# Hi/lo pieces of a token mixer's weights: made in the first feed-forward's input stage and kept in DRAM, instead of beside the projections and the attention that use them

## The chip, the cores and the metric

The kernel runs on one core of one Trainium2 chip. The metric is device microseconds from the start to the end of the launch. The kernel before took 1909.49 us as the median of three runs (1908.7 to 1911.0). The execution that the profile shows took 1910.44 us.

## What is computed

One layer of a hybrid encoder on a sequence of 1024 tokens with 1024 features, all in float32. Three sub-layers follow one another, each with a modulation by a condition vector `c` and a layer norm behind it:

```python
x = post_norm(x, mod[0], 0.5, swiglu(h, ffn1_w_in, ffn1_w_out))
x = post_norm(x, mod[1], 1.0, hybrid_mixer(h, mix_w_in, ..., mix_w_out))
x = post_norm(x, mod[2], 0.5, swiglu(h, ffn2_w_in, ffn2_w_out))
# post_norm: layer_norm(ALPHA*x + w*(1 + gate(c)) * f(x*(1 + scale(c)) + shift(c)))
```

The mixer has one input projection. 1024 of its columns feed a gated unit and a depthwise convolution of width 31; 3 x 512 columns are queries, keys and values of a differential attention (two softmax maps for each of four heads). The two halves are concatenated, and `mix_w_out`, scaled by `1 + gate(c)`, maps them to the output.

## The kernel before

**Arithmetic.** TensorE multiplies in a rounded float32 format. So that the product keeps float32's accuracy, each operand is split into a rounded part `hi` (a copy on ACT) and the rest `lo` (a subtraction on DVE or POOL), and each product is made of three matmuls: hi x hi, hi x lo, lo x hi. `split` (L140) is that pair of instructions. Of a weight that means a load, an ACT copy and a subtraction before TensorE can use it.

**Stages.** Feed-forward 1 has an input stage (`in_phase(0, ...)`, pool `p1a`) and an output stage (`out_phase(0, ...)`, pool `p1b`); then come the mixer's gated unit and its projections (pool `mproj`, `proj_tok` for keys, queries, values), the attention loop over 32 pairs of query block and head (pool `mattn`), the mixer's output projection together with the start of feed-forward 2 (pool `p3a`, `mout`, `play`), and feed-forward 2's input and output stages.

**The input stage** works through 22 column groups j (one group of 128 gate columns and 128 up columns, called a pair below) by a seven-product scheme: for each j, seven products of 12 matmuls, in the order 1, 2, 6, 5, 7, 3, 4. The weights of j + 1 are made while j is multiplied: `in_load` issues four loads on SP's queue into the tiles `ra` and `rb` (two buffers each), `in_gate` splits `ra` into `ah` and `al`, and `in_sums` makes four sums of the raw blocks into the tiles `sf` and splits these into `sh` and `sl`. After each j a function `hook(j)` hangs other work in: at j = 3 `late_consts` (small constants: vectors, convolution taps, rope tables, lambdas), at eight values of j a chunk of the modulation's columns (`ada_cols`), and at 16 and 18 the two halves of gate 0 (`ada_gate`). One such chunk (`ada_chunk`) loads four blocks of 512 KB and takes eight DVE instructions. The heap holds 30 slots of 4 KB per partition, of which the right-hand operands of this stage hold 28.

**The output stage** of feed-forward 1 had a `hook` of its own, which made the two halves of `gate1` (the mixer's gate), with two chunks of the same kind.

**The mixer.** `proj_tok` loads for each of keys, queries and values four blocks of 256 rows (512 KB), splits them into `whi` and `wlo` (four buffers each) and runs two halves of 96 matmuls. Beside them DVE runs the convolution as 120 fused multiply-adds (L949) at the lowest priority, and POOL runs the rope of keys and queries (`rope`, L995 to L998). Before the second half of the values' projection is done, `q_stack(0)` makes the first transposed queries: POOL and DVE split them, TensorE transposes them.

**The attention loop.** For each i: `combine` (POOL: L1128, L1129), `scores(i + 1)` (TensorE, DVE's maximum L1075, ACT's exponential L1077), `flip(i - 1)` (TensorE's transposes), `av(i - 2)`. At i = 22 and i = 26 `out_weights` prepares blocks 0 and 1 of `mix_w_out`: a load, a product with `gate1` on POOL (L1099), an ACT copy and a DVE subtraction. Blocks 2 and 3 follow behind the loop (product on DVE), blocks 4 to 7 in the output projection (`prepare`; DVE for 4 and 5, POOL for 6 and 7).

**Order of the work.** The framework's planner orders each engine's instructions ahead of the run, by the order in which the program names them, by dependencies and by its own model of durations; each engine then runs its list in order. `tc.issue_after(x)` puts the instructions named in its block behind `x` in the list of `x`'s engine; it adds no wait. Each queue of DMAs (SP's, ACT's, POOL's) is issued in order too, and a DMA whose buffer is not free holds up what stands behind it.

## Time and profile before

| | us |
|---|---|
| median of three runs | 1909.49 |
| the profiled execution | 1910.44 |
| its span, from the first to the last instruction | 1908.6 |
| TensorE's matmuls busy | 1825.0 (96% of the span) |
| DVE busy | 1450.6 (76%) |
| ACT busy | 781.3 (41%) |
| POOL busy | 298.2 (16%) |
| mean granted TensorE clock | 0.989 |

An engine's busy time is the union of its instructions' times. A matmul of 512 columns lasts some 0.39 us, and the next one starts 0.23 us after it, so that TensorE counts as busy without a gap where nothing holds it up. The TensorE clock is given as a share of full speed. The profile is of one execution; its times from the span's start are used as places in the text.

### The profile page before, as it was taken

Reading aid. Unit: us, or ns where it says so; the run is one execution under the profiler, and the core shown is the slowest. Engines: PE = TensorE matmul, PEld = TensorE weight load, DVE = VectorE, ACT = ScalarE, POOL = GpSimd, SP = SyncE. Lnnn points to the kernel's source line nnn. Section 1 sums busy time; section 2 is a strip of 40 time slices with the busy share of each in tenths; the row PEclk is TensorE's granted clock in tenths of the full one; section 3 lists DMA queues with packets and bytes.
Section 4 is the critical chain, followed back from the end, with each engine's and each line's share of the span. In section 5 each row is a group of like instructions: output and inputs, shape, how many; then the busy total and the mean of one; then the engine's idle time right before and its main releaser. Section 6 shows DMA issues by size and latency. Waiting matters only on the chain. (4 is left out here: it accounts for less than half of the span.)

```text
span 1908.6 us, 23158 instructions
## 1 busy us (share of the span) xinstructions
PE 1825.0 (96%) x8570; PEld 1513.0 (79%) x8570; DVE 1450.6 (76%) x1952; ACT 781.3 (41%) x1270; POOL 298.2 (16%) x243
## 2 busy tenths in 40 slices
PE   5999999999999999999999789979999999999997
PEld 5788888888888878878788677857888888888886
DVE  4977767766698878999888768688777565569888
ACT  2633333333445442132277664353333333254540
POOL 0000000000000020057667541260000000000001
PEclk9999999999999999999999999989999999999999
DMA  9337445542885325110000014125555333178432
GB/s 311 95 120 224 157 149 177 165 139 90 307 300 157 106 61 166 44 41 27 11 1 1 12 45 154 67 67 170 165 173 180 121 115 123 43 280 284 128 121 72
DMA packets 203952, 246.77 MB, mean 129 GB/s; under 512 B 14378, under 2 KB 125087, under 8 KB 203838
## 3 DMA queue, kind: packets, MB, share of 16 engines
q1 hardware_dynamic: 198378, 234.76, 37.8%
q0 software_dynamic: 2112, 7.34, 1.0%
q10 hardware_dynamic: 3348, 3.18, 0.5%
q8 instruction: 67, 1.10, 0.2%
q14 instruction: 47, 0.39, 0.1%
HBM read 188.08 MB, written 57.15 MB: 128 GB/s over the span
## 5 line engine op out<-in xcount | busy, mean ns | idle before, releaser
L571 PE MATMUL fo<-wr,gl 128*128 128x512 f32 x1848 | 422.5, 390 | 0.5 <-DVE pv L614 0.4
L571 PEld LDWEIGHTS fo<-wr,gl 128*128 128x128 f32 x1848 | 346.2, 188 | 74.7 <-issue 1.0
L142 DVE TENSOR_TENSOR sl<-sf,sh 128x1024 fp32r<-128x1024 f32 x87 | 108.3, 1245 | 110.2 <-ACT sh L141 110.1
L141 ACT CAST sh<-sf 128x1024 fp32r<-128x1024 f32 x88 | 92.8, 1055 | 207.4 <-issue 23.7
L949 DVE SCALAR_TENSOR_TENSOR cacc<-u,convw,cacc 128x1009 f32<-128x1009 f32 (+14 forms) x120 | 151.5, 1324 | 0.2
L381 POOL DMA_DIRECT2D gd<-gf x8 | 4.6, 571 | 887.9 <-DVE gf L447 887.5
L142 DVE TENSOR_TENSOR gl<-gr,gl 128x512 fp32r<-128x512 f32 x148 | 102.1, 695 | 8.5 <-ACT gl L141 6.9
L141 ACT CAST gl<-gr 128x512 fp32r<-128x512 f32 x148 | 90.5, 617 | 24.4 <-DMA gr<-gd 17.6
L155 DVE SCALAR_TENSOR_TENSOR ada<-adaw,c_act,ada 128x512 f32<-128x512 f32 x98 | 73.3, 748 | 28.4 <-DMA adaw<-in_w_ada_dram 27.6
L1075 DVE TENSOR_REDUCE mx<-sc 128x1 f32<-128x1024 f32 x64 | 76.3, 1215 | 19.6 <-PE sc L1073 19.6
L1077 ACT ACTIVATE p<-sc,mx 128x1024 f32<-128x1024 f32 x64 | 71.6, 1121 | 44.7 <-DVE mx L1075 44.5
L141 ACT CAST ah<-ra 128x1536 fp32r<-128x1536 f32 x44 | 65.2, 1481 | 56.0 <-DMA ada<-in_w_ada_dram 12.2
L217 POOL TENSOR_TENSOR rr<-rv,mhalf 128x1 f32<-128x1 f32 x24 | 21.9, 911 | 410.0 <-DVE rv L215 410.0
L409 ACT ACTIVATE gf<-gf 128x512 f32<-128x512 f32 x44 | 27.8, 632 | 125.9 <-DVE gf L408 120.1
L142 DVE TENSOR_TENSOR al<-ra,ah 128x1536 fp32r<-128x1536 f32 x44 | 77.1, 1752 | 1.1 <-ACT ah L141 1.0
L141 ACT CAST wr<-wa 128x512 fp32r<-128x512 f32 x66 | 41.2, 624 | 74.0 <-PE fo L571 72.6
L930 PE MATMUL glu<-hm,gluh 128*128 128x512 f32 x256 | 65.6, 391 | 0.0
L142 DVE TENSOR_TENSOR wr<-wa,wr 128x512 fp32r<-128x512 f32 x66 | 45.6, 690 | 26.1 <-ACT wr L141 25.7
L1129 POOL TENSOR_TENSOR p<-p,p 128x1024 f32<-128x1024 f32 x27 | 65.0, 2408 | 1.8
L1146 PE MATMUL av<-vf,aT 128*128 128x128 f32 x512 | 64.2, 280 | 1.0 <-ACT cacc L1211 1.0
L141 ACT CAST wr<-wb 128x512 fp32r<-128x512 f32 x66 | 40.2, 621 | 60.0 <-PE fo L571 49.6
L1146 PEld LDWEIGHTS av<-vf,aT 128*128 128x128 f32 x512 | 61.3, 196 | 1.5 <-ACT cacc L1211 1.3
(3425 smaller groups left out, 4701.4 us busy)
## 6 DMA issues: line engine op xcount, KB each, us to landing
gr<-gd SPq DMA_DIRECT2D x148, 256.0 KB
ra<-in_ffn_w_in_dram SPq DMA_DIRECT2D x129, 256.0 KB
adaw<-in_w_ada_dram SPq DMA_DIRECT2D x56, 512.0 KB
gd<-gf SPq DMA_DIRECT2D x102, 256.0 KB
wb<-in_ffn_w_out_dram SPq DMA_DIRECT2D x44, 256.0 KB
wa<-in_ffn_w_out_dram SPq DMA_DIRECT2D x44, 256.0 KB
rb<-in_ffn_w_in_dram SPq DMA_DIRECT2D x43, 256.0 KB
gd<-s SPq DMA_DIRECT2D x40, 256.0 KB
```

Of the source, the lines that this page charges most:

```text
L141: a = S.copy(hi, x)
L142: b = eng.tensor_tensor(lo, x, hi.bitcast(F32), ALU.subtract)
L155: V.scalar_tensor_tensor(acc, raw[:, jj], c_act[:, n : n + 1], acc, ALU.mult, ALU.add)
L217: G.tensor_tensor(r, v, mhalf[:, 0:1], ALU.pow)
L409: S.activation(c0, c0, AF.Silu)
L571: PE.matmul(ps, lhsT=g[:, x, ts_], rhs=w[:, y], start=n in (1, 2, 3) and k == i == 0, stop=k == NK - 1 and i == 2, skip_group_check=n not ...
L930: PE.matmul(q[2 * m + h], lhsT=w[:, m * P : (m + 1) * P], rhs=hm[k][h][:, x], start=k == 0 and n == 0, stop=k == KD - 1 and n == 2,)
L949: V.scalar_tensor_tensor(acc[:, lo_t:hi_t], u[:, lo_t + sh : hi_t + sh], convw[:, i, jj : jj + 1], acc[:, lo_t:hi_t], ALU.mult, ALU.add,)
L1075: V.tensor_reduce(mx_, ps, axis=AX.X, op=ALU.max, negate=True)
L1077: S.activation(pe, ps, AF.Exp, bias=mx_, accum_out=sm[:, e : e + 1])
L1129: last = G.tensor_tensor(p0, p0, p1, ALU.add)
L1146: PE.matmul(ps[:, 0:P], lhsT=aT[:, kt], rhs=vf[kt][:, h * P : (h + 1) * P], start=kt == 0, stop=kt == 7)
```

## The change

Five things are done.

1. `mix_load`, `mix_part` and `pieces` are new. In the first input stage they work through 40 units: 24 blocks of 128 x 512 of `mix_w_in` (keys first, then queries, then values) and 16 half blocks of `mix_w_out`. A unit is loaded by POOL's queue into one of two tiles `mw`, multiplied by `gate1` on DVE where it is of `mix_w_out`, copied to hi on ACT, subtracted to lo in place on DVE, and stored by POOL's queue, 512 KB, into the DRAM tensors `mwi` and `mwo`. Two units are loaded after each j from 1 to 10, none after 11, one after 12; from j = 13 two after each j and a third one in the middle of it (after product 5), until they are used up. They are split at the next such place, behind that pair's last DVE and ACT instruction of a product (`pace`).
2. `proj_tok` and `out_weights` load hi and lo from DRAM on SP's queue, and no longer split or multiply anything. Each takes twice the bytes.
3. `gate1` is made in the first input stage, after j = 3 and 5, its loads ordered behind the weight loads on SP's queue. The output stage's hook is gone. Feed-forward 2's gate loads get the same order.
4. `late_consts` moves from j = 3 to j = 11, 12 and 13, in three steps, a step's loads one pair ahead of their use.
5. In feed-forward 1, `ra` and `rb` become one tile `r4`, and the four sums are made in place, in blocks that the gate's split has already read. That frees `sf`, whose place `mw` takes.

```diff
+        if s == 0:
+            r4 = rp.tile([P, 4, 4, P], F32, tag="r4", bufs=2, name=f"r4{s}_{j}")
+            ra, rb = r4[:, 0:3], r4[:, 3]
...
-            q.dma_start(dst, src)
+            pace["Y"] = q.dma_start(dst, src).ins
...
+        if s == 0:
+            for i in order:
+                if i == 0:
+                    eng.tensor_tensor(ra[:, 2], rb, ra[:, 2], ALU.add)
+                    eng.tensor_tensor(rb, ra[:, 0], rb, ALU.subtract)
+                    eng.tensor_tensor(ra[:, 0], ra[:, 2], ra[:, 0], ALU.subtract)
+                else:
+                    eng.tensor_tensor(ra[:, 1], ra[:, 1], ra[:, 0], ALU.subtract)
...
+            last = split(sh, sl, r4[:, i::2] if s == 0 else sf[i])
...
+        hook(1)
         for j in range(2, NJ):
...
                 st[n]()
+                if n == 5 and mid_hook:
+                    mid_hook(j)
...
             hook(j)
+        hook(NJ)
...
+        def mix_load():
+            src, *rest = units.pop(0)
+            t = wp.tile([P, 2, H], F32, tag="mw", bufs=2, name="mw")
+            G.dma_start(t[:, 0], src)
+            loaded.append((t, *rest))
+
+        def mix_part():
+            t, dst, *hs = loaded.pop(0)
+            with tc.issue_after(pace["V"]), tc.issue_after(pace["S"]):
+                if hs:
+                    V.tensor_tensor(t[:, 0], t[:, 0], mods["gate1"][:, hs[0]], ALU.mult)
+                S.copy(t[:, 1].bitcast(F32R), t[:, 0])
+                V.tensor_tensor(t[:, 0].bitcast(F32R), t[:, 0], t[:, 1], ALU.subtract)
+            G.dma_start(dst, t)
...
         def hook(j):
-            if j == 3:
-                late_consts(wp, "ra", 2)
+            if j in gate1_at:
+                n = gate1_at.index(j)
+                if n == 0:
+                    mods["gate1"] = rows.tile([P, D], F32, tag="gate1", name="gate1")
+                with tc.issue_after(pace["Y"]):
+                    todo[j + 1] = ada_gate(wp, raw_slot, 1, 1.0, mods["gate1"], n)
+            if j == 11:
+                todo["consts"] = late_consts(wp, "mw", 2)
+            if 11 <= j <= 13:
+                with tc.issue_after(pace["V"]), tc.issue_after(pace["Y"]):
+                    next(todo["consts"], None)
...
+            pieces({11: 0, 12: 1}.get(j, 2))
+
+        def mid_hook(j):
+            if j > 12:
+                pieces(1)
+
+        def pieces(n):
+            while loaded:
+                mix_part()
+            for _ in range(n):
+                if units:
+                    mix_load()
...
-        def hook(gi, j):
-            if (gi, j) in ((5, 3), (7, 3)):
-                todo1[(7, 2) if gi == 5 else (4, 1)] = ada_gate(wp, raw_ar, 1, 1.0, gate1, int(gi == 7))
...
-                raw = wp.tile([P, 2, H], F32, tag="raw", bufs=3, name=f"{name}r{q}")
-                SY.dma_start(raw, src)
...
-                split(hi, lo, raw)
+                src = mwi[col // H - 2][q * 256 : (q + 1) * 256].rearrange("(k p) x n -> p k x n", p=P)
+                for x, w in enumerate((lo, hi)):
+                    SY.dma_start(w.bitcast(F32), src[:, :, x])
...
-        eng.tensor_tensor(raw, raw, gate1, ALU.mult)
         mo_w[j] = slot(f"moh{j}", (P, D)), slot(f"mol{j}", (P, D))
-        split(*mo_w[j], raw)
+        for w, x in zip(mo_w[j], (1, 0)):
+            SY.dma_start(w.bitcast(F32).rearrange("p (h n) -> p h n", h=2), mwo[j][:, :, x])
...
             if i in (22, 26):
-                with tc.issue_after(last):
-                    out_weights(wp, (i - 22) // 4, G)
+                out_weights((i - 22) // 4)
```

## Rows read from the trace of the kernel before

**Rows 1.** Windows by stage: stretch, length, busy time of each engine, clock, DMA share, GB/s.
```profile
100.00:480.00 380.00, 379.40 (x1700) 313.14 (x1699) 267.03 (x376) 124.31 (x156) 0.00 (x0) 1.00 0.48 153
480.00:700.00 220.00, 219.94 (x973) 180.66 (x972) 182.43 (x304) 105.88 (x179) 11.95 (x17) 1.00 0.59 194
700.00:920.00 220.00, 216.17 (x1010) 178.06 (x1009) 201.27 (x189) 62.79 (x104) 84.92 (x73) 1.00 0.21 67
920.00:945.00 25.00, 20.71 (x93) 16.92 (x92) 21.49 (x19) 4.61 (x8) 14.39 (x12) 0.86 0.00 1
1076.00:1135.00 59.00, 45.46 (x288) 38.65 (x286) 46.12 (x57) 36.07 (x83) 33.43 (x20) 0.91 0.10 33
```

**Rows 2.** Waits of PE between 1076 and 1135: total us, times, longest us.
```profile
PE aT L249 <- POOL p L1129: 6.7, 2, 6.0
```

**Rows 3.** Groups between 1070 and 1200 that write mix_w_out's pieces: busy us, mean ns.
```profile
L142 DVE TENSOR_TENSOR mol<-mor,moh 128x1024 fp32r<-128x1024 f32 x8 | 13.3, 1674 | 1.0 <-ACT moh L141 1.0
L1099 POOL TENSOR_TENSOR mor<-mor,gate 128x1024 f32<-128x1024 f32 x4 | 10.5, 2625 | 30.9 <-DVE x L1319 29.8 <-DVE fl L142 1.1
```

**Rows 4.** Timeline of ACT: first exponentials of scores 8, 20, 22, 23 and 31.
```profile
985.67 1.12 ACT L1077 ACTIVATE p<-sc,mx 128x1024 f32<-128x1024 f32 x1 [0.49 <-DVE mx L1075]
...
1051.96 1.11 ACT L1077 ACTIVATE p<-sc,mx 128x1024 f32<-128x1024 f32 x1 [0.74 <-DVE mx L1075]
...
1067.61 1.11 ACT L1077 ACTIVATE p<-sc,mx 128x1024 f32<-128x1024 f32 x1 [0.40 <-DVE mx L1075]
...
1073.15 1.11 ACT L1077 ACTIVATE p<-sc,mx 128x1024 f32<-128x1024 f32 x1 [0.60 <-DVE mx L1075]
...
1133.38 1.11 ACT L1077 ACTIVATE p<-sc,mx 128x1024 f32<-128x1024 f32 x1 [1.94 <-DVE mx L1075]
```

**Rows 5.** Waits of PE, 100 to 480, then 1135 to 1240.
```profile
PE fi_4S L360 <- ACT p L420: 0.6, 1, 0.6
...
PE mo L1313 <- DVE x L1319: 1.4, 1, 1.4
```

**Rows 6.** Groups of DVE, 866.5 to 940: busy us, mean ns.
```profile
L949 DVE SCALAR_TENSOR_TENSOR cacc<-u,convw,cacc 128x1017 f32<-128x1017 f32 (+14 forms) x50 | 65.2, 1364 | 0.2
L142 DVE TENSOR_TENSOR vl<-vr,vh 128x1024 fp32r<-128x1024 f32 x4 | 5.4, 1346 | 0.0
```

**Rows 7.** Timelines of PE, POOL and DVE between 815 and 965.
```profile
857.14 1.48 PE L1021 MATMUL kT<-ident_r,khl 128*128 128x128 f32 x15 [2.27 <-DVE khl L142]
...
928.40 0.76 PE L1057 MATMUL qTh<-ident_r,qh 128*128 128x128 f32 x4 [2.85 <-POOL qh L1044]
930.60 0.75 PE L1057 MATMUL qTl<-ident_r,ql 128*128 128x128 f32 x4 [1.45 <-POOL ql L1045]
...
822.86 0.32 POOL L996 TENSOR_TENSOR rsk<-kf,ropec 128x64 f32<-128x64 f32 x1
...
873.23 12.88 POOL L995 TENSOR_TENSOR rcq<-qf,ropec 128x128 f32<-128x128 f32 x1 [11.06 <-ACT qf L1027]
...
925.87 1.30 POOL L998 TENSOR_TENSOR qf<-rcq,rsq 128x128 f32<-128x128 f32 x1
...
866.73 17.92 DVE L949 SCALAR_TENSOR_TENSOR cacc<-u,convw,cacc 128x1017 f32<-128x1017 f32 x15
884.57 1.22 DVE L142 TENSOR_TENSOR vl<-vr,vh 128x1024 fp32r<-128x1024 f32 x1
```

**Rows 8.** The page's groups and DMA issues: instructions of the new units' sizes.
```profile
L142 DVE TENSOR_TENSOR gl<-gr,gl 128x512 fp32r<-128x512 f32 x148 | 102.1, 695 | 8.5 <-ACT gl L141 6.9
L141 ACT CAST gl<-gr 128x512 fp32r<-128x512 f32 x148 | 90.5, 617 | 24.4 <-DMA gr<-gd 17.6
L155 DVE SCALAR_TENSOR_TENSOR ada<-adaw,c_act,ada 128x512 f32<-128x512 f32 x98 | 73.3, 748 | 28.4 <-DMA adaw<-in_w_ada_dram 27.6
```

**Rows 9.** Windows in the first input stage, two pairs each, columns as in rows 1.
```profile
220.00:260.00 40.00, 40.00 (x182) 33.23 (x181) 28.12 (x39) 13.29 (x17) 0.00 (x0) 1.00 0.50 161
...
300.00:340.00 40.00, 40.00 (x182) 33.24 (x181) 32.73 (x45) 12.82 (x16) 0.00 (x0) 1.00 0.64 205
```

More of the change, by code (lines that the diff above doesn't have):

```diff
@@ L115, in late_consts @@
         SY.dma_start(cw_raw, a["conv_w"][0])
+        SY.dma_start(ropec, a["rope"].rearrange("(t p) e i -> p t e i", p=P))
+        yield
         cps = bank("consts_ps")
@@ L327, in in_sums @@
     def in_sums(wp, s, j, raws, left, eng=V, order=(0, 1)):
-        ra, rb = raws
+        ra, rb, r4 = raws
         if s == 2 and order == (0, 1) and j in (1, 2):
             eng = G
-        if order[0] == 0:
-            left["sf"] = [wp.tile([P, 2, 4, P], F32, tag="sf", bufs=2, name=f"sf{s}_{j}_{i}") for i in range(2)]
-        sf = left["sf"]
-        if 0 in order:
+        if s == 0:
[4 more added lines that the diff above has]
+                    eng.tensor_tensor(ra[:, 0], ra[:, 2], ra[:, 0], ALU.subtract)
+                else:
+                    eng.tensor_tensor(ra[:, 1], ra[:, 1], ra[:, 0], ALU.subtract)
+        else:
+            sf = [wp.tile([P, 2, 4, P], F32, tag="sf", bufs=2, name=f"sf{s}_{j}_{i}") for i in range(2)]
             eng.tensor_tensor(sf[0][:, 0], rb, ra[:, 2], ALU.add)
             eng.tensor_tensor(sf[0][:, 1], sf[0][:, 0], ra[:, 0], ALU.subtract)
-        if 1 in order:
             eng.tensor_tensor(sf[1][:, 0], ra[:, 0], rb, ALU.subtract)
@@ L342, in in_sums @@
             sl = wp.tile([P, 2, 4, P], F32R, tag="sl", bufs=3, name=f"sl{s}_{j}_{i}")
-            last = split(sh, sl, sf[i])
+            last = split(sh, sl, r4[:, i::2] if s == 0 else sf[i])
             for e in range(2):
-                left[f"S{2 * i + e + 1}"] = (sh[:, e], sl[:, e])
+                n = 2 * i + (1 - e if s == 0 else e) + 1
+                left[f"S{n}"] = (sh[:, e], sl[:, e])
         return last
@@ L512, in in_phase, with out_phase @@
             hook(j)
+        hook(NJ)
         flush()
         return gd
-    def out_phase(s, wp, w_out, gd, gate, xs, done, after, hook):
+    def out_phase(s, wp, w_out, gd, gate, xs, done, after):
         wp.tile([P, H], F32, tag="gr", bufs=4, name="gr_")
@@ L676, in layer_kernel @@
     x_in = a["x"][0]
+    mix_in = a["mix_w_in"][0]
+    mwi = [dram.tile([D, 2, H], F32, name=f"mwi{g}", tag="mwi", bufs=3) for g in range(3)]
+    mwo = [dram.tile([P, 2, 2, H], F32, name=f"mwo{j}", tag="mwo", bufs=8) for j in range(8)]
     with pool("p1a") as wp:
-        in_tags(wp, "ra rb ah al sf sh sl")
+        in_tags(wp, "r4 ah al mw sh sl")
         ops = new_ops()
@@ L829, in layer_kernel @@
         gate_at = (16, 18)
+        gate1_at = (3, 5)
         todo = {}
-        def hook(j):
-            if j == 3:
-                late_consts(wp, "ra", 2)
+        loaded = []
+        def mix_load():
[11 more added lines that the diff above has]
+            G.dma_start(dst, t)
+        units = []
+        for g in (1, 0, 2):
+            for k in range(KD):
+                ks = slice(k * P, (k + 1) * P)
+                units.append((mix_in[ks, (g + 2) * H : (g + 3) * H], mwi[g][ks]))
+        for j in range(8):
+            for h in range(2):
+                hs = slice(h * H, (h + 1) * H)
+                units.append((a["mix_w_out"][0, j * P : (j + 1) * P, hs], mwo[j][:, h], hs))
+        def hook(j):
+            if j in gate1_at:
[9 more added lines that the diff above has]
+                    next(todo["consts"], None)
             if j in cols_at:
@@ L1094, in layer_kernel, with out_weights @@
     mo_w, mo_x = {}, {}
-    def out_weights(wp, j, eng=V, tag="raw", size=D):
-        raw = wp.tile([P, size], F32, tag=tag, bufs=2, name=f"mor{j}")[:, 0:D]
-        SY.dma_start(raw, a["mix_w_out"][0, j * P : (j + 1) * P, :])
-        eng.tensor_tensor(raw, raw, gate1, ALU.mult)
+    def out_weights(j):
         mo_w[j] = slot(f"moh{j}", (P, D)), slot(f"mol{j}", (P, D))
-        split(*mo_w[j], raw)
+        for w, x in zip(mo_w[j], (1, 0)):
+            SY.dma_start(w.bitcast(F32).rearrange("p (h n) -> p h n", h=2), mwo[j][:, :, x])
     def out_feats(j):
@@ L1107, in layer_kernel @@
     with pool("mattn") as wp:
-        wp.tile([P, D], F32, tag="raw", bufs=2, name="raw_")
         featA = [slot(f"featA{h}", (P, T), F32) for h in range(4)]
@@ L1225, in layer_kernel @@
                         next(qs)
-            last = combine(i)
+            combine(i)
             if i + 1 < NI:
```

50 lines of the change are left out of this document (22 added, 28 removed).

## The prediction, made before the changed kernel ran

> **What bounds the kernel now.** I read the windows by stage first [rows 1]. From 100 to 480 (the first input stage) TensorE is busy 379.40 of 380 us at full clock, from 480 to 700 (the first output stage) 219.94 of 220. There only something that makes TensorE wait can change the time. Between 700 and 1135 it does wait: 4.3 us are missing between 920 and 945, at a mean clock of 0.86, and 13.5 us between 1076 and 1135, at 0.91. These are the stages from which the change takes work. The largest wait of the second stretch names POOL [rows 2], the groups beside them the preparation of `mix_w_out` [rows 3]. DVE has room in the input stage (267.03 of 380), ACT more (124.31), POOL is idle, and the DMA engines are 0.48 busy [rows 1].
>
> The sum is made against the profiled execution: 1910.44 us, a span of 1908.6 and 1.8 around it. The median of the runs is 0.95 us below that execution, and the forecast is given as a median. A change below about 0.2%, 3.8 us, can't be told from none.
>
> **Removed: the weights in the attention loop.** At i = 22 and 26 POOL gets a product of some 2.6 us, ACT a copy and DVE a subtraction that averages 1.67 us [rows 3], all in lists that the next scores need; two more products follow on DVE behind them. The price is read from the exponentials' starts [rows 4]. From score 8 to 20 there are 12 steps in 66.29 us, 5.52 each. Scores 20 to 22 take 15.65 us, 4.6 more than two such steps, while the convolution's statistics of the first half run. Scores 23 to 31 take 60.23 us; eight plain steps are 44.2, and the statistics of the second half another 4.6. 11.4 us are left for the weights. TensorE's waits on POOL's sum alone are 6.7 us there [rows 2]; its waits on DVE and the lowered clock behind both add. What comes instead are four DMAs on SP's queue, which has nothing else to issue then, at a DMA share of 0.10 [rows 1]. Taken: -11.4. Bounds: -6.7 (the waits on POOL alone) and -13.5 (all of TensorE's missing time there).
>
> **Removed: the weights in the output projection.** Blocks 2 to 7 lose their products and splits there. TensorE waits once, 1.4 us, for an addition that stands behind them in DVE's list [rows 5]. Taken: -1.4, between 0 and that.
>
> **Removed: the splits of keys, queries and values.** Twelve DVE subtractions of some 1.35 us go (the four of the values stand in [rows 6]; the other eight are alike), and twelve ACT copies. DVE is busy 201.27 of 220 us there [rows 1], but TensorE loses little: one wait of 2.27 us for a split of the keys [rows 7], and 2.85 and 1.45 us before the first transposed queries. These wait for the rope on POOL, whose last instruction ends at 927.2. So the question is what POOL does when DVE has less to do. Its first rope instruction of the queries is there at 873.23 and lasts 12.88 us: DVE runs 15 fused multiply-adds back to back, and POOL ends only after DVE has come to a subtraction of the values' weights (884.57). After that POOL gets one instruction in for each of DVE's, 1.30 us apiece [rows 7]. The change takes away just that subtraction. With the eight subtractions of keys and queries gone, DVE is about 8 x 1.3 / 1.19 = 9 multiply-adds ahead (17.92 / 15 = 1.19 each), so 41 instead of the 50 of [rows 6] are left at 866.7, and an unbroken run lasts until 866.7 + 41 x 1.19 = 915.5. POOL's 32 instructions last 0.32 us where DVE waits (822.86), the wider half of them more; at 0.4 it is 12.8 us: the rope ends near 928.3 where it ended at 927.2. I take 0 for this place: the 2.27 us that TensorE gains before are waited away behind. Bounds: all three waits and the lowered clock back, -8.3 (2.27 + 2.85 + 1.45 + half of 25 x 0.14), and +3.
>
> The Trainium skill (SBUF — State Buffer, section "Who interferes with whom") has it that of a DVE instruction with two SBUF inputs and a POOL instruction that reads SBUF the later one is blocked until the first has finished. The trace agrees from 886.1 on, and differs at 873.23, where nine of DVE's instructions passed before POOL's did; by the page's rule the queries' rope would have no long wait at all, and this place would give -8.3 instead of 0.
>
> The loads that stand in for the splits bring 512 KB twice per block. A block's buffers come free after a quarter of the second half of the projection before, and it is needed three quarters of a half later, 16 us (96 matmuls at 0.23 us are a half); at a DMA share of 0.21 [rows 1] that hides them. Without that cover each block would cost about 3.3 us (1 MB at the 320 GB/s worked out below).
>
> **Added: the units in the input stage.** 40 ACT copies of 0.617 and 40 DVE subtractions of 0.695 us [rows 8], and 16 products of that size: 24.7 us on ACT, 27.8 + 11.1 on DVE. The gate's two chunks bring 16 DVE instructions of 0.75 us, 12 us in all; they leave an output stage in which TensorE lost nothing (219.94 of 220), so nothing comes back there. DVE in sum: 267 + 51 = 318 of 380, so it fits. But not evenly. Two pairs with one chunk between them cost DVE 28.1 of 40 us; from 300 to 340 it is 32.7 [rows 9]. Six units in two pairs add 4.2, and with the products 8.3: 37 to 41 of 40 us. The DMAs are as tight: a share of 0.64 moves 205 GB/s, so 320 is all there is. 300 to 340 has 8.2 MB, and six units add 4.7 MB: 12.9 of the 12.8 MB that 40 us can move. From pair 3 to 6 there is a chunk in every pair now: with the 161 GB/s of a plain stretch, 1 MB more of chunk and 1.6 MB of units per 19 us it is about 298 GB/s.
>
> Lateness there doesn't reach TensorE at once: the next pair's weights are due a pair ahead, and a TensorE product of 2.7 us always lies between an evacuation and its next use. The nearest row is of this stage: DVE's modulation instructions waited 28.4 us for their DMAs over the run [rows 8], and TensorE lost 0.6 us between 100 and 480 [rows 5]. Taken: +3. Bounds: 0, and 64 if nothing at all hid them (24.7 + 27.8 + 11.1); it is near the low end because of that row. In-place sums add a dependency on the gate's split, and let a raw tile go only after its last split; a load still has more than a pair. The one wait of 0.6 us stands where the constants load in the midst of the weights' loads; with the constants moved I take -0.6. POOL's queue has no work of the pairs before the last column, so its waits hold up only the units themselves.
>
> **Sum.** -11.4 - 1.4 + 0 + 3 - 0.6 = -10.4: 1910.44 becomes 1900.0, and as a median 1899.1. I say 1899.
>
> **Rivals.**
> *POOL gets in early* between 873 and 915, at the next of DVE's instructions, as it does from 886 on; it is also what the page named above would make of it. Then the rope ends before TensorE asks for it, and 8.3 us come on top: 1890.8. For it: 40 us of alternating [rows 7]. Against it: the 12.88 us.
> *The units hold up the input stage* (the other side). A unit's load or store is late, its ACT copy stands at the head of ACT's list, and behind it the copy that frees the first product's bank; TensorE stops before its third product. Nineteen pairs carry units, and without them the sum is -13.4. From (13.4 - 3.8) / 19 = 0.5 us per pair the gain can no longer be told, from (13.4 + 3.8) / 19 = 0.9 us the kernel is slower by more than 0.2%; at 1.2 us it takes 1909.5 - 13.4 + 22.8 = 1918.9. For it: DMA and DVE at their limits near 120 to 200 and 300 to 340. Against it: the row on waits, and slack of a pair.
> *The loop's time doesn't fall.* POOL's two instructions and DVE's maximum per step are there still, and the planner orders all of it anew; if only the 1.4 us and a third of the 11.4 come, the time is 1909.5 - 5.2 + 2.4 = 1906.7.
>
> **Chances.** The forecast's own case (1895 to 1905) 0.47, POOL early 0.18, the units 0.24 (half of it within 0.2%, half slower), the loop 0.11. Faster by over 0.2% (below 1905.7): the first two, a little of the others, 0.70. Within: 0.16. Slower: 0.14. The range reaches from 1888, just below POOL early, to 1909, where the units begin to win: about 2 in 10 lie outside.
>
> **What would show it.** In the changed profile: scores 23 to 31 in about 49 us, without POOL products between them; no wait of an addition in the output projection; POOL's first rope instruction of the queries long or short, and TensorE's wait before the first transposed queries; TensorE busy for 376 or more of the input stage's 380 us, and no ACT copy of a unit that waits for a DMA for more than 2.7 us. The prediction is wrong if TensorE shows gaps in each pair from 3 to 6 or from 13 to 19, or if the loop's steps stay at 7 us behind i = 22.

## The result, and the profile after

The changed kernel takes 1921.61 us (median of 7 runs, 1918.82 to 1927.04), the kernel before in the same runs 1910.96. The ratio is 1.0056, with a 95% interval from 1.0047 to 1.0066: slower by over 0.2%, where 1899 us and a range of 1888 to 1909 were forecast. The profiled execution took 1921.73 us with a span of 1920.0.

The windows by stage of the changed kernel, columns as in [rows 1], stages moved by what was lost before them (stretch, length, busy time of TensorE, of its weight loads, of DVE, ACT and POOL, clock, DMA share, GB/s):

```profile
100.00:300.00 200.00, 200.00 (x899) 165.21 (x898) 165.04 (x231) 76.11 (x103) 19.63 (x36) 1.00 0.77 253
300.00:480.00 180.00, 162.30 (x682) 129.84 (x681) 132.35 (x200) 59.02 (x81) 21.74 (x40) 0.95 0.65 218
520.00:728.00 208.00, 207.95 (x925) 171.45 (x924) 168.33 (x279) 100.97 (x171) 11.59 (x17) 1.00 0.52 168
728.00:962.00 234.00, 226.41 (x1055) 186.49 (x1054) 199.94 (x190) 52.76 (x96) 96.67 (x84) 0.99 0.26 86
1105.00:1160.00 55.00, 50.79 (x380) 46.09 (x381) 39.14 (x59) 46.24 (x107) 27.82 (x18) 1.00 0.33 116
```

Up to 300 TensorE is busy all the time, at a DMA share of 0.77: two units a pair and the gate's chunks after pairs 3 and 5 hold up nothing, though DVE has 165.04 of 200 us to do and the DMA engines carry 253 GB/s. Between 300 and 480 17.7 us are missing, at a lower DMA share and with less for DVE to do. That is where constants are loaded (pairs 11 to 13) and three units a pair are made (from pair 13 on). In the tail of the attention TensorE now misses 4.2 of 55 us where it missed 13.5 of 59, at full clock instead of 0.91.

The table gives, for this kernel and the experiments, what each stretch lost (+) or gained (-) against the kernel before, in us. It is worked out from the traces: the start of TensorE's first matmul of a stage, less the same start before, and the differences of these from boundary to boundary. "Pair 13" is the way from pair 12's to pair 13's sums; "scores" runs to the output projection's first matmul, the last column to TensorE's last matmul of the kernel. A row is one execution, the profiled one. It lies within 1.6 us of its kernel's median, but 4.0 us above it in e9 and 2.6 in e11, so as much in these two rows may be that execution's own. e3, e8 and e12 are not in the table.

| kernel | up to pair 5 | 5 to 12 | pair 13 | 13 to the end of the stage | first output stage | projections, to the first score | scores | output projection | second feed-forward |
|---|---|---|---|---|---|---|---|---|---|
| changed | -0.7 | 0.9 | 5.5 | 23.8 | -1.8 | -0.5 | -16.3 | -2.5 | 2.7 |
| e1 | 5.2 | 5.7 | 0.0 | 20.0 | -1.8 | -0.6 | -16.2 | -2.6 | 9.1 |
| e2 | 0.8 | 1.2 | 5.7 | 2.4 | 8.9 | -0.7 | -16.3 | -2.5 | 5.5 |
| e4 | 2.4 | 1.8 | 0.0 | 2.2 | -1.8 | -0.2 | -16.2 | -2.5 | 5.4 |
| e5 | -0.1 | 0.9 | 3.4 | 28.1 | -1.8 | -6.0 | -16.2 | -2.5 | 5.9 |
| e6 | -0.1 | 0.9 | 0.7 | 0.9 | -1.8 | 1.2 | -17.6 | -2.5 | 5.6 |
| e7 | -0.5 | 0.9 | 0.7 | 0.7 | -1.8 | -4.9 | -15.6 | -2.5 | 3.6 |
| e9 | 0.7 | 1.1 | 0.7 | 2.2 | -1.8 | -0.6 | -0.1 | 2.0 | 9.6 |
| e10 | 3.0 | 1.8 | 0.2 | 2.3 | -1.8 | -6.1 | -16.2 | -2.6 | 10.1 |
| e11 | 1.6 | 5.9 | 0.7 | 11.4 | -1.8 | -0.6 | -16.2 | -2.5 | 6.7 |
| e13 | 0.5 | 3.0 | 7.8 | 6.0 | 8.8 | -0.8 | -16.3 | -2.5 | 1.2 |
| e14 | 20.1 | 0.9 | 0.7 | 21.4 | -1.8 | -0.6 | -16.3 | -2.5 | 2.8 |

In the changed kernel the input stage costs 29.5 us; everything behind it gives 18.4 back. (1.8 of both is work that only moved: the first output stage had four TensorE matmuls for `gate1`, 2.0 us of busy time, and they stand in the input stage now.) The loop gains more than forecast, the input stage takes ten times what was set for it.

**Who waits in the input stage.** The waits between 300 and 500, all engines (total us, times, longest):

```profile
POOL mwo L871 <- DVE mw L870: 62.8, 12, 8.1
...
POOL mw L860 <- DMA mwo<-mw: 40.3, 14, 5.6
ACT mw L869 <- DVE mw L868: 29.9, 7, 7.1
...
DVE mw L868 <- DMA mw<-in_mix_w_out_dram: 19.5, 10, 6.3
...
PE fi_18A L374 <- ACT p L417: 4.2, 1, 4.2
```

Read from below it is a ring (L417 is ScalarE's copy of a product out of its bank). TensorE waits for ScalarE's copy L417, which frees a product's bank. That copy stands behind a unit's copy (L869), which waits for the unit's product on DVE (L868), which waits for the unit's load. The load (L860) was issued late, because its tile still had to be stored, and the store (L871) because DVE had come late to the subtraction. One turn of it, and TensorE's first matmuls of pairs 17 to 19 (timelines of POOL, DVE, ACT and PE):

```profile
402.21 0.54 POOL L871 DMA_DIRECT2D mwo<-mw  x1 [3.60 <-DVE mw L870]
405.23 0.54 POOL L871 DMA_DIRECT2D mwo<-mw  x1 [2.47 <-DVE mw L870]
408.72 0.55 POOL L860 DMA_DIRECT2D mw<-in_mix_w_out_dram  x1 [2.95 <-DMA mwo<-mw]
411.83 0.55 POOL L860 DMA_DIRECT2D mw<-in_mix_w_out_dram  x1 [2.56 <-DMA mwo<-mw]
417.56 0.54 POOL L871 DMA_DIRECT2D mwo<-mw  x1 [5.18 <-DVE mw L870]
...
434.74 0.55 POOL L860 DMA_DIRECT2D mw<-in_mix_w_out_dram  x1 [5.64 <-DMA mwo<-mw]
...
459.34 0.55 POOL L860 DMA_DIRECT2D mw<-in_mix_w_out_dram  x1 [5.05 <-DMA mwo<-mw]
...
412.19 0.75 DVE L158 SCALAR_TENSOR_TENSOR ada<-adaw,c_act,ada 128x512 f32<-128x512 f32 x1 [4.12 <-DMA adaw<-in_w_ada_dram]
413.54 0.69 DVE L868 TENSOR_TENSOR mw<-mw,gate 128x512 f32<-128x512 f32 x1 [0.59 <-DMA mw<-in_mix_w_out_dram]
...
414.31 0.62 ACT L869 CAST mw<-mw 128x512 fp32r<-128x512 f32 x1 [5.77 <-DVE mw L868]
414.83 0.58 ACT L417 COPY p<-fi_17A 128x512 f32<-128x512 f32 x1
...
407.08 0.39 PE L374 MATMUL fi_17A<-r_0bh,ah 128*128 128x512 f32 x1
...
415.46 0.57 PE L374 MATMUL fi_17A<-r_0t1h,sh 128*128 128x512 f32 x1 [2.78 <-ACT p L417]
...
431.70 0.39 PE L374 MATMUL fi_18A<-r_0bh,ah 128*128 128x512 f32 x1
...
457.99 0.79 PE L374 MATMUL fi_19A<-r_0bh,ah 128*128 128x512 f32 x1
```

A tile that is stored at 402.21 is loaded again at 408.72 and stored again at 417.56: 15.35 us a round. That is no fixed time: from 340 on the rounds last 9.3 to 24.5 us, and with three units a pair on two tiles a round is two thirds of a pair on average, however long the pair has become. What decides is which unit comes late. The loads at 408.72, 434.74 and 459.34 are those of the third units of pairs 16, 17 and 18, which are handed out in the middle of the pair and are to be split at its end. Each waits for the store of a unit that was split in that same middle, and each is issued only when the next pair's matmuls have begun (407.08, 431.70, 457.99). From the middle to the end there are three products of 2.7 us, 8.2 us; a store and a load, from issue to landing, take 4.8 and 4.0 us in the median from 340 on, with the split to be done ahead of them. As an estimate from these numbers, a third unit can't be there in time with two tiles. With two units a pair each has a whole pair. TensorE stops ahead of its third product, as the rival said, and the matmuls after the stop last 0.63 us instead of 0.39 at first (the window from 400 to 420 has a mean granted clock of 0.91, some of it at the lower level).

**The constants.** TensorE between pairs 12 and 13:

```profile
312.30 0.26 PE L120 MATMUL consts_ps<-ident,vec_raw 45*128 45x45 f32 x1
315.59 0.40 PE L124 MATMUL convw_ps<-ident,cw_raw 31*128 31x31 f32 x4 [3.03 <-DMA cw_raw<-in_conv_w_dram]
320.36 0.95 PE L182 MATMUL adac<-ones,ada 128*128 128x1 f32 x8
321.30 0.50 PE L374 MATMUL fi_13A<-r_0bh,ah 128*128 128x512 f32 x1
```

The constants are loaded into the units' two tiles, whose stores were only issued at 301.15; TensorE, in order, comes to pair 13 at 321.30 instead of 315.54: it waits 3.03 us for the taps, and the matmuls behind that wait are slower at first.

**The stages that gain.** The first exponentials of scores 8, 20, 22, 23 and 31, beside [rows 4]:

```profile
1012.81 1.12 ACT L1135 ACTIVATE p<-sc,mx 128x1024 f32<-128x1024 f32 x1 [0.49 <-DVE mx L1133]
...
1079.03 1.11 ACT L1135 ACTIVATE p<-sc,mx 128x1024 f32<-128x1024 f32 x1 [0.74 <-DVE mx L1133]
...
1094.33 1.11 ACT L1135 ACTIVATE p<-sc,mx 128x1024 f32<-128x1024 f32 x1
...
1100.25 1.11 ACT L1135 ACTIVATE p<-sc,mx 128x1024 f32<-128x1024 f32 x1 [0.79 <-DVE mx L1133]
...
1144.36 1.11 ACT L1135 ACTIVATE p<-sc,mx 128x1024 f32<-128x1024 f32 x1 [1.95 <-DVE mx L1133]
```

Scores 8 to 20 take 66.22 us (66.29 before), 20 to 22 15.30 (15.65), and 23 to 31 44.11 instead of 60.23: eight plain steps of 5.5.

**Queries.** POOL's first rope instruction, DVE beside it, and TensorE's two waits, where [rows 7] has 12.88, 17.92, 2.85 and 1.45:

```profile
899.54 39.12 POOL L1053 TENSOR_TENSOR rcq<-qf,ropec 128x128 f32<-128x128 f32 x1 [12.26 <-ACT qf L1085]
...
894.24 50.89 DVE L1008 SCALAR_TENSOR_TENSOR cacc<-u,convw,cacc 128x1015 f32<-128x1015 f32 x42
...
956.40 0.75 PE L1115 MATMUL qTh<-ident_r,qh 128*128 128x128 f32 x4 [4.53 <-POOL qh L1102]
957.64 0.75 PE L1115 MATMUL qTl<-ident_r,ql 128*128 128x128 f32 x4 [0.49 <-POOL ql L1103]
```

### The profile page after: what moved, and what is told of

It is laid out like the page before. It is cut to its first block, busy times and chain, and to the rows that moved or that the text cites. A ratio compares the mean times of both kernels' runs of the same rounds, so it can differ in the third digit from the quotient of the medians.

```text
span 1920.0 us, 23453 instructions
## 1 busy us (share of the span) xinstructions
PE 1830.6 (95%) x8570; PEld 1515.1 (79%) x8570; DVE 1446.8 (75%) x1984; ACT 782.0 (41%) x1290; POOL 327.5 (17%) x319
## 5 line engine op out<-in xcount | busy, mean ns | idle before, releaser
L1008 DVE SCALAR_TENSOR_TENSOR cacc<-u,convw,cacc 128x1012 f32<-128x1012 f32 (+14 forms) x120 | 146.6, 1286 | 0.2
L145 DVE TENSOR_TENSOR sl<-sf,sh 128x1024 fp32r<-128x1024 f32 x43 | 54.5, 1268 | 65.4 <-ACT sh L144 65.2
L144 ACT CAST gl<-gr 128x512 fp32r<-128x512 f32 x148 | 90.4, 617 | 22.9 <-DMA gr<-gd 16.2
L144 ACT CAST sh<-sf 128x1024 fp32r<-128x1024 f32 x44 | 46.4, 1054 | 106.4 <-PE fi_17S L374 5.8
L158 DVE SCALAR_TENSOR_TENSOR ada<-adaw,c_act,ada 128x512 f32<-128x512 f32 x98 | 73.2, 747 | 16.3 <-DMA adaw<-in_w_ada_dram 15.6
L424 ACT ACTIVATE gf<-gf 128x512 f32<-128x512 f32 x44 | 27.8, 631 | 96.3 <-DVE gf L423 93.4
L444 ACT ACTIVATE gf<-gf 128x512 f32<-128x512 f32 x44 | 27.7, 629 | 94.3 <-DVE gf L443 94.3
L145 DVE TENSOR_TENSOR sl<-r,sh 128x1024 fp32r<-128x1024 f32 x44 | 53.6, 1221 | 14.6 <-ACT sh L144 14.3
L1130 PE MATMUL sc<-kst,qTh 128*128 128x512 f32 x128 | 54.1, 423 | 7.1 <-ACT p L1135 7.0
```

What stands on the lines that cost most here:

```text
L144: a = S.copy(hi, x)
L145: b = eng.tensor_tensor(lo, x, hi.bitcast(F32), ALU.subtract)
L158: V.scalar_tensor_tensor(acc, raw[:, jj], c_act[:, n : n + 1], acc, ALU.mult, ALU.add)
L1008: V.scalar_tensor_tensor(acc[:, lo_t:hi_t], u[:, lo_t + sh : hi_t + sh], convw[:, i, jj : jj + 1], acc[:, lo_t:hi_t], ALU.mult, ALU.add,)
L1130: PE.matmul(ps[:, ks], lhsT=qTh[:, m], rhs=kst[m][:, ks], start=True, stop=False)
```

## The experiments

Medians of each kernel, and ratios to the kernel before on the same chip; stages are in the table. The diffs are against the changed kernel.

**e1: the constants back after pair 3.**

```diff
-            if j == 11:
-                todo["consts"] = late_consts(wp, "mw", 2)
-            if 11 <= j <= 13:
...
+            if j == 3:
+                for _ in late_consts(wp, "r4", 2):
+                    pass
```

> The constants are loaded and transposed in one go after pair 3 again, through the tiles of the raw weights; the 40 units stay as the change has them. Theory of the constants: TensorE's stall ahead of pair 13 (5.76 us in the changed kernel) is the constants' own, because their tiles come from the two buffers of the units; 0.6 us of waiting comes back at pair 3, and the kernel takes 1921.6 - 5.2 = 1916.4 us. Rival: the units' buffers were late by then anyway, and the stall only moves to the next pair: 1921 us.

1927.96 us, 1.0091 [1.0076, 1.0106]. The stall at pair 13 is gone (0.0), but 10.9 us are lost up to pair 12, beside the gate's chunks and the units, where the constants had cost 0.6 before. Both times missed (1916.4 and 1921 us): the constants' stall is their own, but the place that they had before is dear now.

**e2: no third unit.**

```diff
-            pieces({11: 0, 12: 1}.get(j, 2))
+            pieces({11: 0}.get(j, 2))
...
-            if j > 12:
-                pieces(1)
+            pass
```

> No unit in the middle of a pair: two units a pair up to pair 21 (none at pair 11), constants at 11 to 13 as in the changed kernel. Theory of the two buffers: three loads, splits and stores a pair don't pass through two tiles (a load waits for the store before it, the gate product waits for the load at the head of VectorE's list, the copy behind it at the head of ScalarE's); with two a pair nearly all of the 23.8 us lost in pairs 14 to 20 comes back: about 1900 us. Rival, the gate product as such: the 16 units with a product hold up VectorE at any rate, so about a third comes back: 1913 us. Rival, DMA: the engines are full; nothing much changes: 1919 us.

1914.97 us, 1.0018 [1.0009, 1.0027]. Pairs 13 to 21 lose 2.4 us instead of 23.8, products and all. The run takes away the third unit and the place in the middle of the pair together, so it doesn't tell the two apart. But the last units now come so late that they head ScalarE's list at the start of the output stage, ahead of its casts, and 10.7 us go there. ACT and PE in that place (timeline, then a wait):

```profile
513.23 0.62 ACT L869 CAST mw<-mw 128x512 fp32r<-128x512 f32 x1 [8.38 <-DVE mw L868]
...
PE fo L590 <- ACT gl L144: 7.7, 1, 7.7
```

**e3: the units' tiles from the 30 shared slots.**

```diff
-            t = wp.tile([P, 2, H], F32, tag="mw", bufs=2, name="mw")
+            t = slot("mw", dt=F32)
```

> The units' tiles come from the 30 slots shared by the kernel and no longer from two buffers of their own (which only the constants use now); number and order of the units as in the changed kernel. Theory of the two buffers: neither the loads of the units nor those of the constants wait for a store, the input stage loses under 5 us instead of 29.5: about 1897 us. Rival, DMA or the product itself: only the constants' 5.7 us come back: 1916 us.

1985.53 us, 1.0387 [1.037, 1.0405]. The shared slots are short in this stage: SP's loads of the columns' chunks now wait for the units' stores, 66.5 us in all:

```profile
SPq L167 <- DMA mwi<-mw: 66.5, 18, 8.3
```

So the run tells nothing of the two tiles, only that there was no room beside them; it missed by 88 us.

**e4: the output projection's units alone**, one a pair from pair 6, constants after pair 3; keys, queries and values split in the projections as before.

```diff
-        for g in (1, 0, 2):
...
-            pieces({11: 0, 12: 1}.get(j, 2))
+            pieces(int(j >= 6))
...
+                split(hi, lo, raw)
```

> Only the 16 units of the output projection's weights are made ahead, one a pair from pair 6 on; keys, queries and values are loaded raw and split in the projections as before; constants after pair 3 as before. Theory: the gain of the attention loop (15.8 us between the two traces) and of the output projection (2.5) hangs on these units alone, the input stage loses 0 to 2, the start of the second input stage loses 2.7: 1909.5 - 15.8 - 2.5 + 2.7 + 1 = 1895 us. Rival: part of the 15.8 us comes from the projections' splits (scores that start with a freer VectorE): 1900 us or more.

1902.8 us, 0.9957 [0.9942, 0.9972]. Scores -16.2 and output projection -2.5, as with all 40 units. It misses 1895 by the input stage's 6.4 where 1 was set (two thirds of it up to pair 12, where the constants are again), and the second feed-forward's 5.4 where 2.7 was set.

**e5: the queries' rope on VectorE.**

```diff
-        def rope(x, t, name):
+        def rope(x, t, name, G=G):
...
-            rope(qf[t], t, "q")
+            rope(qf[t], t, "q", V)
```

> The changed kernel, with the 32 rope instructions of the queries on VectorE in place of POOL. Theory: in the changed kernel POOL's first rope instruction of the queries lasts 39.12 us because VectorE's convolution leaves it no gap, and TensorE's waits of 4.5 and 0.5 us before the first transposed queries, with the lowered clock behind them, hang on that alone: 1921.6 - 6 = 1915.6 us, and the first score starts 5 to 8 us earlier after the keys' projection than it did. Rival: POOL's copies of the queries, which stay, wait just as long, or VectorE ends its convolution so much later (32 x 0.25 = 8 us) that the first maximum is late: 1921 us or more.

1921.54 us, 1.0056 [1.0041, 1.0071]: the same time as the changed kernel. The stages say otherwise: the way to the first score gains 5.5 us over the changed kernel, as expected, and the input stage happens to lose 2.8 more, the second feed-forward 3.2 more. TensorE's waits on POOL are gone. Whether the later two are chance of the order or of the run isn't told by this.

**e6: the output projection's units away from the constants**, splits of keys, queries and values as before.

```diff
-            pieces({11: 0, 12: 1}.get(j, 2))
+            pieces({6: 2, 7: 2, 8: 2, 9: 2, 14: 2, 15: 1, 16: 1, 17: 1, 18: 2, 19: 1}.get(j, 0))
```

> Only the 16 units of the output projection's weights: two a pair after pairs 6 to 9, none while the constants are loaded after pairs 11 to 13, the last eight after pairs 14 to 19, none in the middle of a pair. Keys, queries and values are split in the projections as before. Theory: nothing waits for a unit's tile, the constants' stall of 5.7 us is gone, the input stage loses 2 us or less; with 15.8 us from the attention loop, 2.5 from the output projection, 1.8 from the gate that leaves the first output stage, and 2.7 to 4.5 lost in the second input stage: 1893 us. Rival: the constants at pair 13 stop TensorE for 5.7 us wherever the units are: 1899 us.

1898.55 us, 0.9937 [0.9922, 0.9952]. The input stage loses 2.4 us in all, and pair 13 0.7 instead of 5.5: the constants cost next to nothing where their tiles are free.

**e7: e6 with e5's rope.**

> The kernel of the units apart, with the 32 rope instructions of the queries on VectorE as well. Theory: TensorE's waits for the first transposed queries (2.85 and 1.45 us in the kernel before) go and the clock stays up: 5 us less than the units apart, 1888 us. Rival: VectorE, which still splits the weights of the projections here, has no room for 8 us more: the same as the units apart or slower.

1891.94 us, 0.9909 [0.9891, 0.9926]: faster than both kernels. Against e6 the way to the first score is 6.1 us shorter, of which the scores give 2.0 back. The other 2.0 of the gain stand in the second feed-forward, which the rope doesn't touch. TensorE's waits between 780 and 1000 name POOL no more:

```profile
PE sc L1125 <- ACT p L1130: 3.6, 5, 1.3
PE kT L1074 <- DVE khl L145: 2.6, 2, 2.3
```

**e8 and e14: the units' instructions on POOL.** e14 keeps the two `issue_after`, e8 has none. They name instructions of DVE and ACT and order only those engines' lists, so in neither are the units held to their places: the first 20 are stored up to 137.1 us (e14) and 138.0 (e8), from 8 us on, where the changed kernel stores them from 122.5 to 301.7. The edit of e14:

```diff
-                    V.tensor_tensor(t[:, 0], t[:, 0], mods["gate1"][:, hs[0]], ALU.mult)
-                S.copy(t[:, 1].bitcast(F32R), t[:, 0])
-                V.tensor_tensor(t[:, 0].bitcast(F32R), t[:, 0], t[:, 1], ALU.subtract)
+                    G.tensor_tensor(t[:, 0], t[:, 0], mods["gate1"][:, hs[0]], ALU.mult)
+                G.tensor_scalar(t[:, 1].bitcast(F32R), t[:, 0], 1.0, 0.0, ALU.mult, ALU.add)
+                G.tensor_tensor(t[:, 0].bitcast(F32R), t[:, 0], t[:, 1], ALU.subtract)
```

> The changed kernel with its 40 units at the same places and through the same two buffers, but with product, copy and subtraction of a unit all on POOL: 96 instructions that no longer stand in the lists of VectorE and ScalarE. Theory of the lists: TensorE stops in pairs 14 to 20 because a unit that waits for its load stands at the head of VectorE's and ScalarE's lists; on POOL it holds up only other units, so those pairs lose under 8 us instead of 23.8, and the constants' 5.7 us at pair 13 stay or grow: about 1905 us. Rival, DMA: the pairs' own loads are what is late; the time stays near 1921 us. Rival, contention: POOL's instructions slow VectorE's down, or POOL is too late with the units: over 1921 us.

> The changed kernel with product, copy and subtraction of every unit on POOL, three units a pair from pair 13 on, through the same two buffers, now placed behind the pair's own evacuations as in the changed kernel. Theory of the lists: nothing of a unit stands in VectorE's or ScalarE's list, so pairs 14 to 20 lose under 8 us, where the constants' 5.6 us at pair 13 stay. Rival, POOL and VectorE in each other's way: the pairs lose 10 us or more, and VectorE's instructions beside POOL's are longer than the 0.69 us of a 128x512 addition alone.

e8 took 1936.81 us, 1.0137 [1.0116, 1.0157]; e14 1935.44 us in one run beside 1913.45. Both lose some 20 us up to pair 5 already, where those 20 units now run, and 21.4 to 22.7 from pair 13 on (e8's profiled execution is 7.0 us above its median). DVE's and ACT's lists are free of units and the time is as bad. That fits the rival, by which POOL and DVE are in each other's way, but doesn't show it alone: DVE's waits for the columns' chunks have doubled too, and the units run at other times. So the theory of the lists had no clean test here. Groups of DVE between 300 and 500, e14 first, then the changed kernel:

```profile
L158 DVE SCALAR_TENSOR_TENSOR ada<-adaw,c_act,ada 128x512 f32<-128x512 f32 x35 | 33.0, 943 | 10.6 <-DMA adaw<-in_w_ada_dram 10.6
L342 DVE TENSOR_TENSOR r<-r 128x512 f32<-128x512 f32 x10 | 9.2, 922 | 0.1
```

```profile
L158 DVE SCALAR_TENSOR_TENSOR ada<-adaw,c_act,ada 128x512 f32<-128x512 f32 x33 | 24.6, 746 | 5.4 <-DMA adaw<-in_w_ada_dram 5.3
L342 DVE TENSOR_TENSOR r<-r 128x512 f32<-128x512 f32 x9 | 6.2, 684 | 0.0
```

**e9: the units of keys, queries and values alone**, two a pair after pairs 1 to 9 and 14 to 16.

```diff
+            pieces(2 * (j <= 9) + 2 * (14 <= j <= 16))
...
+    def out_weights(wp, j, eng=V, tag="raw", size=D):
...
```

> Only the 24 units of keys, queries and values, two a pair after pairs 1 to 9 and 14 to 16, constants after pairs 11 to 13; the output projection's weights are made in the attention loop and behind it as before. Theory: the splits of keys, queries and values are worth nothing, since the rope on POOL takes the place of every wait that goes; 1.8 us come from the gate that leaves the first output stage, 1 to 3 are lost in the input stages: 1909 to 1912 us. Rival: VectorE's room in the projections is worth several us later on (the convolution ends earlier): 1905 us.

1920.55 us, 1.0044 [1.0027, 1.006]: they bring 0.6 us up to the first score and nothing in the scores. That part is as the theory has it. The time is 9 us above the kernel before. In the profiled execution, which took 4.0 us more than the median, 9.6 us are lost in the second feed-forward (below).

**e10: 32 units (keys, queries and the output projection; values as before), two a pair after pairs 4 to 19, constants after pairs 1 to 3, rope on VectorE.**

```diff
-            if j == 11:
+            if j == 1:
...
-            if 11 <= j <= 13:
+            if 1 <= j <= 3:
...
-            pieces({11: 0, 12: 1}.get(j, 2))
+            pieces(2 * (4 <= j <= 19))
```

> 32 units (keys, queries, output projection; values raw), two a pair after pairs 4 to 19, constants loaded and used after pairs 1 to 3, rope of the queries on VectorE. Theory: at two a pair and with the constants away from the units' buffers the input stage loses 2 us or less; the attention loop, the output projection, the rope and the waits for the keys' splits give 15.8 + 2.5 + 5 + 2: 1889 us. Rival: two units a pair beside the chunks of the columns are more than the lists of VectorE and ScalarE hold, as the constants after pair 3 were: 1897 us or more.

1899.74 us, 0.9935 [0.992, 0.995]. The gains are as forecast (-6.1, -16.2, -2.6). The input stage loses 7.3 and the second feed-forward 10.1, so it misses 1889 and is no better than e6.

**e11: four tiles**, room taken from the sums' splits.

```diff
-            sh = wp.tile([P, 2, 4, P], F32R, tag="sh", bufs=3, name=f"sh{s}_{j}_{i}")
...
+            sh = wp.tile([P, 2, 4, P], F32R, tag="sh", bufs=2 if s == 0 else 3, name=f"sh{s}_{j}_{i}")
...
-            t = wp.tile([P, 2, H], F32, tag="mw", bufs=2, name="mw")
+            t = wp.tile([P, 2, H], F32, tag="mw", bufs=4, name="mw")
```

> The changed kernel with four tiles for the units (and the constants) instead of two; the room comes from the splits of the sums in the first input stage, which get two tiles each instead of three. Number, order and places of the units, three a pair from pair 13 on, as in the changed kernel. Theory of the two buffers: a unit's load no longer waits for the store of a unit before it, so the 23.8 us of pairs 14 to 20 shrink to 8 or less and the constants' 5.6 us at pair 13 go; a few us may be lost where the sums have one tile less: 1905 us or less. Rival, DMA (three units a pair are more than the engines move beside the pairs' own loads): pairs 14 to 20 lose 15 us or more still: 1915 us or more.

1913.57 us, 1.0002 [0.999, 1.0014]. Pair 13 loses 0.7 instead of 5.5, the pairs behind it 11.4 instead of 23.8: two tiles more take away half of it. Up to pair 12 this kernel loses some 7 us more than the changed one; its sums with fewer tiles may be the reason, there and in part of the 11.4 too, but that was not run alone. What stays isn't the ring alone. DVE is full in places and waits for the columns' chunks, 17.8 us in 11 waits (window, then wait):

```profile
380.00:400.00 20.00, 19.69 (x90) 15.76 (x89) 19.60 (x32) 8.63 (x12) 2.74 (x5) 1.00 0.81 269
...
DVE ada L158 <- DMA adaw<-in_w_ada_dram: 17.8, 11, 3.9
```

**e12 and e13: e2 and the third unit's traffic alone**, three copies of 256 KB a pair within DRAM. e12 read a weight, which was ready at any time, and the copies were all issued between 3.0 and 26.1 us; e13 reads stored products, and its copies come three at 302.6 us and then six at a time beside every second pair.

```diff
+                for x in range(3):
+                    G.dma_start(idle[j - 13][x], pace["gd"][2][(j - 2) // 2])
```

> The kernel of two units a pair, and in the middle of pairs 13 to 19, where the third unit stood, only traffic: three copies of 256 KB each from DRAM to DRAM on POOL's queue, without a tile, a product, a copy or a subtraction. Theory of the two buffers and the lists: traffic alone holds up nothing; pairs 14 to 21 lose 2 to 5 us as with two units a pair: 1915 to 1918 us. Rival, DMA: the third unit's 768 KB a pair are what made the loads late; pairs 14 to 20 lose 15 us or more: 1928 us or more.

> The kernel of two units a pair, and beside pairs 13 to 19 three copies of 256 KB each from DRAM to DRAM per pair, now held to their places, since each reads a product that was stored a pair or two before (left to themselves they had all run in the first 26 us). Theory of the two buffers and the lists: traffic alone, without a tile or an instruction on VectorE and ScalarE, holds up little: pairs 14 to 21 lose 2 to 6 us, and the kernel takes 1915 to 1919 us. Rival, DMA: the third unit's traffic is what makes the loads late: pairs 14 to 21 lose 15 us or more, 1928 us or more.

e12 took 1931.67 us, 1.0109 [1.0092, 1.0126]: 16 us lost at the start, and no test of the question. e13 took 1918.45 us in one run beside 1913.45. From pair 13 on it loses 6.0 us instead of e2's 2.4, with DMA shares as high as in the changed kernel or higher:

```profile
340.00:360.00 20.00, 20.00 (x90) 16.57 (x89) 15.92 (x26) 7.32 (x10) 4.65 (x9) 1.00 0.91 293
360.00:380.00 20.00, 19.82 (x92) 16.17 (x90) 13.74 (x21) 5.89 (x9) 3.28 (x6) 1.00 0.83 278
```

So traffic is worth 3.6 of the 21.4 us by which three units a pair lose more than two, or 7.2 if all that e13's input stage loses more than e2's is put down to it; both from one run.

## Why the prediction was wrong, step by step

**The step that failed** is the price of the units in the input stage: "Taken: +3", and with it "-0.6" for the constants. It was 29.5 us. The reason given for +3 was that lateness doesn't reach TensorE at once, since a product of 2.7 us lies between an evacuation and its next use, and that POOL's waits "hold up only the units themselves". The trace shows the opposite: a unit's copy kept ScalarE waiting for 5.77 us up to 414.31, longer than a product, and TensorE stood for 2.78 us behind it. 5.5 of the 29.5 are the constants, which no step priced as users of the units' tiles (e1 and e6: 0.0 and 0.7 without that meeting). 23.8 belong to pairs 13 to 21 with three units a pair. The prediction summed DVE's time and DMA's bytes over two pairs and put the tight places at 120 to 200 and 300 to 340. The first lost nothing. In the second, by the change's own order, hardly a unit is under way (none is loaded after pair 11, one after 12), so the six units counted there belong behind it. What it left out is the round of a tile: load, product, copy, subtraction, store, two transfers and three lists long. A third unit in two tiles gets its tile only after the store of a unit of the same half pair, and its load is issued when the unit is already due. With two units a pair 2.4 us are lost (e2), with four tiles 11.4 (e11), and the third unit's traffic is worth 3.6 to 7.2 (e13). The split of what is left with four tiles, between DVE's load, DMA's lateness and the sums' fewer tiles, was not settled, and the third unit at another place than the middle of the pair was not run. The Trainium skill (Trainium Kernel Development and Optimization, section "Best Practices") recommends double buffers to overlap DMA with compute. The runs agree for two units a pair (2.4 us lost) and not for three (23.8, and 11.4 with four tiles): a tile that is filled, worked on in place and emptied has two transfers in its round, and here two buffers didn't cover both within half a pair.

**The rival of the units** had the mechanism right: a unit's copy heads ScalarE's list, the copy behind it frees the bank, TensorE stops before its third product. It spread the price, 1.2 us a pair over 19 pairs; in fact it was next to nothing up to pair 12 (0.2 us) and 3.4 us a pair, on average, on the last seven where units were made (23.8 / 7). Its total, 1918.9 us, comes near the 1921.61 measured, in part by luck: the loss was spread wrongly and the loop gave more than the sum had.

**The attention loop** gave 16.3 us where 11.4 were taken and 13.5 were the bound. The step was mis-sized by the 4.6 us set aside for the convolution's statistics of the second half: scores 23 to 31 take 44.11 us, eight plain steps, so the statistics cost nothing there and the whole 16.1 us were the weights. The bound counted only the time in which TensorE stood (13.5 of 59 us); the granted clock in that stretch rose from 0.91 to 1.00 as well. e4 shows that the 16 units of the output projection alone bring it, e9 that the other 24 bring none of it.

**The output projection** gave 2.5 for 1.4: the wait of [rows 5] is gone, and no wait at all is left there.

**Keys, queries and values** were taken at 0 and measured at -0.5. The step was right in its course too, the number with some luck. POOL's rope ends at 955.18 in the changed kernel; less the 27.7 us by which the projections start later it is 927.5, where 928.3 was forecast and 927.2 was before. DVE's run ended at 945.1 (917.4 without the 27.7), 1.9 us later than forecast, and POOL had come in at 938.62 already, with five instructions done or begun before the end of the run. e9 gives 0.6 for these units alone, and e5 and e7 show what stood in the way: with the rope off POOL the same stretch gains 5.5 to 6.1.

*POOL gets in early* is refuted for these instructions: the first was blocked for 39.12 us, beside some 33 multiply-adds of DVE (39.12 / 1.19). The keys' rope, shortly before, did get in beside DVE's multiply-adds, at 0.71 to 1.44 us an instruction from 872.15 on; what made the difference is open. The Trainium skill (SBUF — State Buffer, section "Who interferes with whom") has the later of two such instructions blocked until the first has finished. Here POOL's first one waited on through 33 of DVE's, so the trace differs from it.

**First output stage.** "Nothing comes back there" was off by 1.8 us. Every kernel in which the gate's two chunks moved shows it (in e2 and e13 under the 10.7 us that late units cost there). Before, four matmuls for the gate stood there, 2.0 us of TensorE's busy time; in the changed kernel there is none. They are in the input stage now, so nothing was gained by that.

**Second feed-forward.** Not priced; it loses 2.7 us in the changed kernel and 1.2 to 10.1 in the experiments. 1.2 of the 2.7, and 2.5 to 7.0 us in the nine kernels that lose 3.6 us or more, are lost in pair 9, where DVE's modulation instruction waits for its chunk. The change does touch this: its third point orders feed-forward 2's gate loads behind the weight loads. The chunk's first load before and after, and DVE's wait for a later one after (SP's and DVE's timelines):

```profile
1429.11 0.38 SPq L164 DMA_DIRECT2D adaw<-in_w_ada_dram  x1
...
1443.78 0.94 SPq L167 DMA_DIRECT2D adaw<-in_w_ada_dram  x2
...
1458.09 1.54 DVE L158 SCALAR_TENSOR_TENSOR ada<-adaw,c_act,ada 128x512 f32<-128x512 f32 x2 [3.06 <-DMA adaw<-in_w_ada_dram]
```

Pair 9 begins at 1437.35 before and at 1446.93 after, so the loads start 8.2 us ahead of it before and 3.2 us after. That the new order is the cause is likely and not shown: no run put the old one back, and the loss differs from kernel to kernel.

## What to carry to other kernels

Work that is moved under a full TensorE is not priced by free engine time and bytes alone: take one buffer through its whole round, up to the store that frees it, and ask whether the next piece can be loaded into it before that piece is due. Where it can't, the late load reaches the main engine through the lists of the engines that share its evacuations; here two units a pair throughout (e2, a ratio of 1.0018) beat three at the end (1.0056), even with 10.7 us lost because its last units came late. And find the part of a change that carries the gain: here 16 of 40 units brought what the loop and the output projection gained, and with them alone, kept away from the constants, and the rope off POOL, the kernel takes 1891.94 us.

## What the runs showed of the hardware

One POOL instruction with two SBUF operands lasted 39.12 us beside back-to-back DVE multiply-adds. The five behind it, still beside DVE's run, took 1.29 to 1.43 us each, and once that run had ended the same instructions took 0.32 to 0.46. The other way round, beside POOL's 128x512 instructions for the units (e14, between 300 and 500), DVE's own 128x512 instructions went on average from 684 to 922 ns and from 746 to 943 ns. An idle POOL beside a busy DVE was no free engine here.
